# Two matmuls with a gelu between them: the first weight range cast on other engines, one table load, x of three pairs earlier, phase two's reads moved

## The chip, the cores and the metric

One core of a Trainium2 chip. The metric is the device time of one execution in microseconds (us).

## The reference

```python
x: (8, 1024, 1024) float32, w1: (1024, 4096), w2: (4096, 1024)
h = x @ w1
h = 0.5 * h * (1 + np.tanh(np.sqrt(2 / np.pi) * (h + 0.044715 * h ** 3)))
return (h @ w2).astype(np.float32)
```

## The kernel before

**Phase one** makes `gelu(x @ w1)` and writes it in float16 to memory; **phase two** reads it back transposed and multiplies it by w2. All engines run in the order in which the program is written out by hand (a manual schedule): each engine takes its own instructions strictly in that order, and waits where an operand or a buffer isn't ready. Casts to float16 are scaled: a chunk of x by a measure of its rows, a weight range by its largest value.

x is 8192 rows, taken as 64 *chunks* c of 128 rows, two of which make a *pair* k (32 pairs). w1's columns are taken in four *ranges* r; range 0 is loaded as eight *halves* n (`load_w1(0, n)`), of which 0 to 3 belong to one block of columns and 4 to 7 to the other.

A chunk goes through these steps: `load_x`, `look_x` (ScalarE, sums magnitudes, L190), `scale_x` (VectorE, L193 and L197), `cast_x` (L179 on VectorE, L177 on GpSimd), then `turn_x_pe`: eight transposes on TensorE into the PSUM tile `turned` (L216) and a copy from there into `xT[k]` (L221 on ScalarE, L223 on VectorE). A half of w1: `look_w1` (its largest value; VectorE L150, or ScalarE L285), `widest_w1` and `scale_w1` (largest over all halves of a block, through one transpose on TensorE, L162), `cast_w1`. `factors_of_block` makes the few numbers with which products are scaled back.

The first six pairs (FIRST) are multiplied plainly with range 0, the first one also with range 1. This is cut into 28 *quarters* p of 8 matmuls (L401): a half of the pair's rows against one block of columns. Pairs 0 and 1 take quarters 0 to 7, pair 2 takes 8 to 11, pair 3 12 to 15, pair 4 16 to 19, pair 5 20 to 23; 24 to 27 are pair 0 with range 1. After each quarter comes a gelu on ScalarE (L441) and a cast on GpSimd (L177) into a tile `g2`; a store to memory follows on the SP queue when both casts of a tile are made (L450). Steps for later pairs are placed in the quarters by a table, `early(p, step, ...)`: they are emitted after quarter p. The function `between` emits steps in the middle of quarters 0, 1 and 3.

The remaining products of phase one run in *units* (a pair and a range), by a scheme with seven products instead of eight; a unit's methods are m1 to m7 (TensorE) and g21, g11, g22, g12 (gelus). They are spread over three units' time, and each unit has seven slots for background work.

Phase two takes each pair in 26 *products* s, whose left sides are sums (`sum_g`, VectorE, L171) of tiles that DMA transposes bring (`load_g`, L548, on the SP queue), and whose right sides are tiles made from w2 and fetched on the SP queue (L395). `take` reads a product's bank: the first read of an output quarter is ScalarE's (L573), the later ones VectorE's (L569). The last two units of phase one share their time with the first products: `extra()` emits three products, twice in a unit.

Tiles of several kinds (the junk that a look writes, `x16`, `e`, `g2`, the sums `gs`) share one ring of 11 buffers, `k2`, handed out in order of allocation; the casts `g` of the units share 8.

Of the kernel before, what the change touches and what calls it, by code (L numbers as in the profile page):

```python
# [10 lines left out]
ACT = mybir.ActivationFunctionType  # L11
# [68 lines left out]
def kernel(  # L80
# [60 lines left out]
    ratio = small.tile([P, 2], F32, name="ratio")  # L141
# [5 lines left out]
    V, S, G = nc.vector, nc.scalar, nc.gpsimd  # L147

    def absmax(dst, src):
        V.tensor_reduce(  # L150
            out=dst, in_=src, op=ALU.max, axis=AX.X, apply_absolute_value=True
        )
# [20 lines left out]
    def cast(eng, o, i, s):  # L173
        if eng is S:
            S.activation(out=o, in_=i, func=ACT.Copy, scale=s)
        elif eng is G:
            G.tensor_scalar(out=o, in0=i, scalar1=s, scalar2=1.0, op0=ALU.mult, op1=ALU.mult)  # L177
        else:
            V.tensor_scalar(out=o, in0=i, scalar1=s, scalar2=None, op0=ALU.mult)  # L179
# [8 lines left out]
    def look_x(c):  # L188
        junk = k2.tile([P, H], mybir.dt.bfloat16, name="junk", tag="k2")
        S.activation(out=junk, in_=xraw[c], func=ACT.Abs, accum_out=xl[:, c:c + 1])  # L190
# [50 lines left out]
    def times(o, a, s, eng=V):  # L241
        if eng is G:
            G.tensor_scalar(out=o, in0=a, scalar1=s, scalar2=1.0, op0=ALU.mult, op1=ALU.mult)
        else:
            V.tensor_scalar(out=o, in0=a, scalar1=s, scalar2=None, op0=ALU.mult)
# [8 lines left out]
    def factors_of_block(k, block, eng):  # L254

        c, b = slice(2 * k, 2 * k + 2), slice(NR + block, NR + block + 1)
        times(up[:, block, c], xm[:, c], w1m[:, b], eng)
        times(rt[:, c] if block else rs[:, k, :, 0], xi[:, c], w1j[:, b], eng)
# [12 lines left out]
    def load_w1(r, n, pool=wpool, tag="w"):  # L271
        b, half = BLOCKS[n // 2], n % 2
        row = (b in (B21, B22)) * HK * P + half * 2 * P
        col = (b in (B12, B22)) * I // 2 + r * N
        wraw[r, n] = pool.tile([P, 2, N], F32, name="wn", tag=tag)
        (G if r else nc.sync).dma_start(
            out=wraw[r, n],
            in_=w1[row:row + 2 * P, col:col + N].rearrange("(c p) n -> p c n", p=P),
        )

    def look_w1(r, n, eng=V):
        src, dst = wraw[r, n].rearrange("p c n -> p (c n)"), w1c[:, r, n:n + 1]
        if eng is S:
            junk = k2.tile([P, 2 * N], mybir.dt.bfloat16, name="junk", tag="k2")
            S.activation(out=junk, in_=src, func=ACT.Abs, scale=1.0 / SPAN, accum_out=dst)  # L285
        else:
            absmax(dst, src)
# [29 lines left out]
    def cast_w1(r, n, eng):  # L317
        b, half = BLOCKS[n // 2], n % 2
        if (r, b) not in w1set:
            w1set[r, b] = wpool.tile([P, HK, N], F16, name="w", tag="w")  # L320
        c = r or NR + n // 4
        cast(eng, w1set[r, b][:, 2 * half:2 * half + 2], wraw.pop((r, n)), w1i[:, c:c + 1])
# [296 lines left out]
    NQ = len(order)  # L619
    todo = {}  # L620

    def plan(u, slot, f, *args):
        assert 0 <= u, (f, args)
        todo.setdefault((u, slot), []).append((f, args))
# [6 lines left out]
    def early(p, f, *args):  # L631
        plan(p // 4, p % 4, f, *args)

    early(1, turn_x_pe, 3, S)
    for k in range(2, FIRST):
        for h in range(2):
            c = 2 * k + h
            p = (4, 7, 11, 14)[k - 2] + h
            early(p - 1, look_x, c)
            early(p, scale_x, c)  # L640
            early(p, cast_x, c, V)
            if h:
                early(p, factors_of_block, k, 0, V)
                early(p, factors_of_block, k, 1, G)
            if k > 3:
                early((2, 5)[k - 4], load_x, c, wpool, "w")
            early(4 * k - 2 + 2 * h, turn_x_pe, c, V if h else S)
    for k in first:
        for i in range(4):
            if k == 1:  # L650
# [16 lines left out]
    for r in range(2, NR):  # L667
        u = (r - 1) * FIRST - 1
# [24 lines left out]
    for k in list(middle) + list(last):  # L693
        a = at[k] if k in middle else at[last[0]]
        for h in range(2):
            c = 2 * k + h
# [10 lines left out]
    u = at[middle[0]] - 1  # L707
# [22 lines left out]
    for i, node in enumerate(FORMS):  # L730
        r, n = divmod(i, 7)
# [6 lines left out]
    def unit(u, extra):  # L738
        q = now.get(u)
        p1, p2 = now.get(u - 1), now.pop(u - 2, None)  # L740
        if u < NQ:
            q = now[u] = Quad1(*order[u])
            q.m1()
        background(u, 0)
        if p1:
            p1.m7()
        if p2:
            p2.g21()
        if p1:
            p1.g11()  # L750
        let_go(len(held) - 2 if len(held) > 2 else 0)
        if u >= NQ:
            extra()
        background(u, 1)
        if p2:
            p2.m3()
        background(u, 2)
        if u < NQ:
            q.m2()
        background(u, 3)  # L760
        if u < NQ:
            q.m6()
        if p1:
            p1.g22()
        if p2:
            p2.g12()
        let_go(len(held) - 2 if len(held) > 2 else 0)
        background(u, 4)
        if u < NQ:
            q.m5()  # L770
        background(u, 5)
        if p1:
            p1.m4()
        if u >= NQ:
            extra()
        background(u, 6)

    with tc.manual_schedule(
        engines={
            mybir.EngineType.PE, mybir.EngineType.Activation, mybir.EngineType.DVE,  # L780
            mybir.EngineType.Pool, mybir.EngineType.SP,
        }
    ):
        load_x(0, wpool, "w")
        for n in range(4):
            load_w1(0, n)
        make_identity(nc, identity)
        V.tensor_copy(out=identity16, in_=identity)
        for c in range(1, 4):
            load_x(c, wpool, "w")  # L790
        for n in range(4, 8):
            load_w1(0, n)
        for c in range(4, 8):
            load_x(c, wpool, "w")
        look_x(0)
        scale_x(0)
        cast_x(0, S)
        t = x16[0]
        turn_x_pe(0, S)
        warm_up(t, WARM)  # L800
        for n in range(4):
            look_w1(0, n)
        widest_w1(0, 0)
        for c in range(1, 4):
            look_x(c)
        scale_w1(NR)
        warm_up(t, 12)
        cast_w1(0, 0, V)
        cast_w1(0, 1, G)
        scale_x(1)  # L810
        cast_x(1, V)
        cast_w1(0, 3, G)
        cast_w1(0, 2, V)
        factors_of_block(0, 0, G)
        plain = {(k, 0): Plain(k, 0) for k in range(FIRST)}
        plain[0, 1] = Plain(0, 1)
        quarters = [(k, 0, half, s) for s in range(2) for k in range(2) for half in range(2)]
        quarters += [(k, 0, half, s) for k in range(2, FIRST) for half in range(2) for s in range(2)]
        quarters += [(0, 1, half, s) for half in range(2) for s in range(2)]

        def between(p):
            if p == 0:
                turn_x_pe(1, V)
                look_w1(0, 4, S)
                scale_x(2, 2)
                cast_x(2, V)
                cast_x(3, G)
                factors_of_block(1, 0, G)
            elif p == 1:
                turn_x_pe(2, V)  # L830
                look_w1(0, 5, S)
                look_w1(0, 6)
                look_w1(0, 7)
                widest_w1(0, 1)
            elif p == 3:
                scale_w1(NR + 1)
                for n in (4, 5, 6, 7):
                    cast_w1(0, n, G if n % 2 else V)
                for k in range(2):
                    factors_of_block(k, 1, V)  # L840

        for p, (k, r, half, s) in enumerate(quarters):
            plain[k, r].quarter(half, s, ("pa", "pc")[p % 2], lambda: between(p))
            for j in (p % 4,) if p % 4 < 3 else (3, 4, 5, 6):
                background(p // 4, j)
            let_go(len(held) - 1 if len(held) > 1 and p % 2 else 0)
        now = {}
        for u in range(FIRST + 1, NQ):
            unit(u, None)
        V.tensor_scalar(  # L850
            out=vo, in0=xm, scalar1=w2n, scalar2=SPAN, op0=ALU.mult, op1=ALU.mult
        )
        V.tensor_scalar(out=vn, in0=vo, scalar1=-1.0, scalar2=None, op0=ALU.mult)
        for u in range(NQ, NQ + 2):
            unit(u, lambda: second(3))
        let_go()
        for u in range(NQ + 2, NQ + 6):
            for slot in range(7):
                background(u, slot)
        assert not todo, todo.keys()  # L860
        second(NP * len(PRODUCTS) - done[0])
# [28 lines left out]
```

## Time and profile before

| | |
|---|---|
| median of 3 runs | 1542.61 us (1542.05 to 1543.32) |
| profiled execution | 1542.97 us, its span 1541.1 us |
| TensorE busy | 1521.2 us, 99% |
| VectorE, ScalarE, GpSimd busy | 77%, 47%, 32% |
| ScalarE's table loads | 2, of 1.28 us, at 0.74 and 18.29 |
| first product of a quarter | 14.20 us |
| phase two's first product | 806.24 us |

The profile calls TensorE PE (PEld its weight loads), VectorE DVE, ScalarE ACT, GpSimd POOL, SyncE's DMA queue SPq. In a timeline a line has the start, the time from the first start to the last end, the engine, the line of the program, the operation, output <- input with sizes and type, and in brackets how long the engine stood idle before it and what ended that. Ends of matmuls are modelled: starts are exact, so a wait of TensorE is read best from starts.

### The profile page before, as it was taken

The numbers are of one execution on the slowest core, as the hardware profiler recorded it, in microseconds if no ns is written. First come the engines' busy times: TensorE is split into PE (matmuls) and PEld (weight loads), VectorE is DVE, ScalarE is ACT, GpSimd is POOL, SyncE is SP. The second block draws the span as 40 slices with busy tenths as digits, with TensorE's granted clock in tenths as the row PEclk, the third lists the DMA queues.
The fourth block names the chain that finished last, engine by engine and source line by source line (L and its number), as shares of the span: only waits on it lengthen the run. The fifth ranks groups of instructions, "written<-read, shape, count | busy, mean of one in ns | idle before, by whom it ended". The sixth has DMA issues, their size and how long they took to land. (4 is left out here: it accounts for less than half of the span.)

```text
span 1541.1 us, 28626 instructions
## 1 busy us (share of the span) xinstructions
PE 1521.2 (99%) x10408; PEld 1014.7 (66%) x10408; DVE 1181.5 (77%) x2413; ACT 731.6 (47%) x1296; POOL 488.2 (32%) x593
## 2 busy tenths in 40 slices
PE   7999999999999999999999999999999999999999
PEld 4444444444444444444448888888888888888888
DVE  6786787777877777675248888888888888888886
ACT  6778777777777777797662111111111111111111
POOL 5778654566656666554442000000000000000000
PEclk9999999999999999999999999999999999999999
DMA  9654989878788887883699668668767767866872
GB/s 333 225 173 145 267 270 312 248 228 229 233 260 239 244 262 211 251 219 104 216 267 235 136 123 165 129 132 151 142 135 136 151 132 129 165 131 123 157 141 80
DMA packets 459806, 293.93 MB, mean 191 GB/s; under 512 B 333840, under 2 KB 427024, under 8 KB 459664
## 3 DMA queue, kind: packets, MB, share of 16 engines
q1 hardware_dynamic: 456208, 279.52, 71.6%
q0 software_dynamic: 3456, 12.58, 2.6%
q8 instruction: 81, 1.33, 0.4%
q14 instruction: 61, 0.50, 0.1%
HBM read 96.99 MB, written 114.29 MB: 137 GB/s over the span
## 5 line engine op out<-in xcount | busy, mean ns | idle before, releaser
L401 PEld LDWEIGHTS <-gs 128*128 128x128 f16 x4608 | 450.7, 98 | 54.7 <-DVE gs L171 1.4
L177 POOL TENSOR_SCALAR g<-e,rs 128x512 f16<-128x512 f32 x448 | 366.1, 827 | 279.6 <-ACT e L453 240.2
L401 PEld LDWEIGHTS <-xs 128*128 128x128 f16 x1936 | 189.4, 98 | 230.9 <-issue 3.5
L168 DVE TENSOR_TENSOR e<-pc,e 128x512 f32<-128x512 f32 x242 | 161.6, 686 | 204.9 <-ACT e L519 203.5
L401 PEld LDWEIGHTS <-xT 128*128 128x128 f16 x1676 | 163.5, 98 | 201.3 <-issue 4.6
L401 PE MATMUL pa<-w,gs 128*128 128x256 f16 x2304 | 288.3, 273 | 1.2 <-ACT o L573 1.2
L401 PE MATMUL pa<-w,xT 128*128 128x512 f16 x1080 | 256.4, 379 | 5.0 <-ACT xT L221 2.0
L453 ACT ACTIVATE e<-e,us 128x512 f32<-128x512 f32 x363 | 249.2, 719 | 6.8 <-DVE e L168 6.8
L401 PE MATMUL pa<-w,xs 128*128 128x512 f16 x968 | 248.4, 379 | 2.4 <-ACT e L500 2.4
L401 PE MATMUL pc<-w,xs 128*128 128x512 f16 x968 | 248.4, 379 | 0.0
L401 PEld LDWEIGHTS <-gT 128*128 128x128 f16 x2048 | 200.3, 98 | 23.7 <-DMA w<-wd 0.5
L573 ACT ACTIVATE o<-pa,vo 128x256 f32<-128x256 f32 x96 | 45.3, 472 | 332.7 <-PE pa L401 332.7
L401 PE MATMUL pc<-w,gs 128*128 128x256 f16 x1536 | 193.8, 273 | 0.2 <-DMA w<-wd 0.2
L401 PE MATMUL pa<-w,gT 128*128 128x256 f16 x1024 | 132.7, 273 | 0.2 <-DMA w<-wd 0.2
L401 PE MATMUL pb<-w,xT 128*128 128x512 f16 x484 | 124.2, 379 | 0.0
L569 DVE SCALAR_TENSOR_TENSOR o<-pc,vo,o 128x256 f32<-128x256 f32 x160 | 77.0, 482 | 58.5 <-PE pc L401 58.5
L510 ACT COPY e<-pa 128x512 f32<-128x512 f32 x121 | 70.9, 586 | 90.4 <-PE pa L401 85.0
L171 DVE TENSOR_TENSOR gs<-gT,gs 128x1024 f16<-128x1024 f16 x160 | 109.3, 683 | 1.5 <-POOL g L177 0.7
L569 DVE SCALAR_TENSOR_TENSOR o<-pa,vo,o 128x256 f32<-128x256 f32 x192 | 92.0, 480 | 19.6 <-PE pa L401 19.6
L401 PE MATMUL pb<-w,gs 128*128 128x256 f16 x768 | 99.5, 273 | 0.0
L401 PE MATMUL pc<-w,gT 128*128 128x256 f16 x768 | 99.5, 273 | 0.0
L500 ACT COPY e<-pa 128x512 f32<-128x512 f32 x121 | 70.0, 579 | 50.5 <-PE pa L401 50.5
(100 smaller groups left out, 1451.4 us busy)
## 6 DMA issues: line engine op xcount, KB each, us to landing
gd<-g SPq DMA_DIRECT2D x484, 128.0 KB, 3.2
wn<-in_w_dram SPq DMA_DIRECT2D x72, 512.0 KB, 5.5
xn<-in_x_dram SPq DMA_DIRECT2D x64, 512.0 KB, 5.6
out_dram<-o SPq DMA_DIRECT2D x62, 512.0 KB, 3.7
w<-wd SPq DMA_DIRECT2D x25, 512.0 KB, 6.3
wn<-in_w_dram POOLq DMA_DIRECT2D x24, 512.0 KB, 5.7
wd<-wt SPq DMA_DIRECT2D x24, 512.0 KB, 5.1
gd<-g SPq DMA_DIRECT2D x14, 256.0 KB, 5.0
```

The lines of the kernel that those rows point to most:

```text
L168: V.tensor_tensor(out=o, in0=a, in1=b, op=ALU.add)
L171: V.tensor_tensor(out=o, in0=a, in1=b, op=ALU.subtract)
L177: G.tensor_scalar(out=o, in0=i, scalar1=s, scalar2=1.0, op0=ALU.mult, op1=ALU.mult)
L401: nc.tensor.matmul(bank, lhsT=left(i), rhs=right[i], start=start and i == 0, stop=i == n - 1, skip_group_check=True,)
L453: S.activation(out=e, in_=src, func=ACT.Gelu_apprx_tanh, scale=self.u[half][s])
L500: S.copy(self.e11, self.pa)
L510: S.copy(self.e12, self.pa)
L569: V.scalar_tensor_tensor(out=o, in0=ps, scalar=v, in1=o, op0=ALU.mult, op1=ALU.add)
L573: S.activation(out=o, in_=ps, func=ACT.Copy, scale=v)
```

## The change

Five edits. (1) Halves 1 and 3, and later 5 and 7, of w1's range 0 are cast on ScalarE instead of GpSimd; the look at chunk 3 goes behind the first two of these casts, the look at half 4 from ScalarE to VectorE, and the factors of block 1 for pairs 0 and 1 from VectorE to GpSimd. (2) A gelu of two numbers per partition is ScalarE's first instruction. (3) Looks, scales and casts of x are emitted one quarter earlier for pair 3 and two for pairs 4 and 5. (4) The turns of pairs 3 to 5 are emitted one quarter earlier. (5) In the two last units the first group of phase two's products, with its sums, reads, and the DMA transposes that it issues for pair 1, goes ahead of the gelus g21 and g11 and of the stores released with them.

```diff
@@ table of early steps
-            p = (4, 7, 11, 14)[k - 2] + h
+            p = (4, 6, 9, 12)[k - 2] + h
...
-            early(4 * k - 2 + 2 * h, turn_x_pe, c, V if h else S)
+            early(4 * k - 2 + 2 * h - (k > 2), turn_x_pe, c, V if h else S)
@@ def unit
         if p1:
             p1.m7()
+        if u >= NQ:
+            extra()
         if p2:
             p2.g21()
         if p1:
             p1.g11()
         let_go(len(held) - 2 if len(held) > 2 else 0)
-        if u >= NQ:
-            extra()
         background(u, 1)
@@ start
+        V.memset(ratio, 0.0)
+        S.activation(out=ratio, in_=ratio, func=ACT.Gelu_apprx_tanh)
         make_identity(nc, identity)
...
-        for c in range(1, 4):
-            look_x(c)
+        look_x(1)
+        look_x(2)
         scale_w1(NR)
         warm_up(t, 12)
         cast_w1(0, 0, V)
-        cast_w1(0, 1, G)
+        cast_w1(0, 1, S)
         scale_x(1)
         cast_x(1, V)
-        cast_w1(0, 3, G)
+        cast_w1(0, 3, S)
         cast_w1(0, 2, V)
+        look_x(3)
@@ def between
                 turn_x_pe(1, V)
-                look_w1(0, 4, S)
                 scale_x(2, 2)
                 cast_x(2, V)
                 cast_x(3, G)
                 factors_of_block(1, 0, G)
+                look_w1(0, 4)
...
                 for n in (4, 5, 6, 7):
-                    cast_w1(0, n, G if n % 2 else V)
+                    cast_w1(0, n, S if n % 2 else V)
                 for k in range(2):
-                    factors_of_block(k, 1, V)
+                    factors_of_block(k, 1, G)
```

## The prediction

> **What bounds the kernel now.** The page first: part 1 gives TensorE (PE) 99% of the span, part 2 a granted clock of 9 in every slice. So only the time in which PE stands still can be won, and the second view, PE's waits, says where that is (us in total, times, longest):
>
> ```profile
> PE 1521.2 (99%) x10408; PEld 1014.7 (66%) x10408; DVE 1181.5 (77%) x2413; ACT 731.6 (47%) x1296; POOL 488.2 (32%) x593
> ...
> PEclk9999999999999999999999999999999999999999
> ```
>
> ```profile
> PE turned L216 <- ACT x L175: 7.2, 1, 7.2
> PE pa L401 <- ACT e L500: 2.4, 4, 1.0
> PE pa L401 <- ACT xT L221: 2.0, 1, 2.0
> PE pa L401 <- DVE w L179: 1.7, 2, 0.9
> PE pa L401 <- ACT o L573: 1.2, 1, 1.2
> PE pa L401 <- POOL w L177: 1.0, 3, 0.4
> PE pa L401 <- DVE xm L193: 0.3, 1, 0.3
> PE pc L401 <- ACT xT L221: 0.3, 1, 0.3
> PE pc L401 <- DMA w<-wd: 0.2, 1, 0.2
> PE pa L401 <- DMA w<-wd: 0.2, 1, 0.2
> ```
>
> Matmul ends are modelled, so I take the lost time from starts. In the timeline four 512-wide matmuls without a wait take 0.863 us from start to start, eight 1.727, eight transposes 0.437. By these, PE loses 4.2 us in quarters 0 to 4 (14.20 to 28.47), 2.16 ahead of quarter 16, 3.0 at four places in the units (76.55, 93.80, 107.07, 131.88, all on L500's copies), and in phase two 1.36 at 814.57 and 0.39 + 0.40 at 831.54 and 832.81. The first product, at 14.20, is not moved by the change: its cast waits for the same chain of maxima.
>
> The timeline around the largest of these:
>
> ```profile
> 47.56 0.69 ACT L441 ACTIVATE e<-pc,up 128x512 f32<-128x512 f32 x1 [1.71 <-DMA gd<-g]
> 50.79 1.00 ACT L221 COPY xT<-turned 128x1024 f16<-128x1024 f16 x1
> 51.85 1.90 PE L401 MATMUL pa<-w,xT 128*128 128x512 f16 x8 [2.00 <-ACT xT L221]
> ```
>
> ScalarE (ACT) stood 1.71 us for a buffer that a store held, then had a look, a look of w1 and two gelus ahead of the copy that quarter 16 needs.
>
> **First range, quarters 0 to 3.** Before: halves 1 and 3 are cast on GpSimd (POOL) in 1.59 us each, and beside it VectorE's casts take 1.16 and 1.60 instead of the 0.75 of rows without it. After: ScalarE is free at 14.11 (its second look), casts half 1 in 1.15 (L175's rows: 1.15, 1.16) to 15.27, half 3 starts 1.05 later and ends at 16.32; VectorE ends half 2 at 15.85. Quarter 0 ends at 17.08 instead of 18.04: 0.96 ahead. Little of that stays. The look at chunk 3 now stands behind both casts (16.22, before 14.24), VectorE's scale of chunks 2 and 3 waits for it (17.39, before 17.64), and then the look at half 4 (1.21) that ScalarE gave up stands on VectorE ahead of the copy of turned chunk 2: 19.58 to 20.27. Quarter 2 starts at 20.33 instead of 20.66.
>
> The table load (1.28 at 18.29) leaves ScalarE; the built program of the change has one load, at its head, where ScalarE idles until x lands at 4.42 anyway, and that also hides the memset and the 128x2 gelu. Gelu of quarter 0 goes at 17.38, chunk 3's copy ends at 21.69, ahead of the end of quarter 2: quarter 3 starts at 22.06 instead of 22.84. Its first half ends at 22.92, the transpose of the maxima follows at 23.28 (spread is ready at 23.10, as before; it then waited for PE until 23.71), and the casts of halves 4 to 7 start at 24.40 instead of 24.81. VectorE at 0.75 and ScalarE at 1.05 apart have them ready at 25.15, 25.55, 25.82 and 26.60; quarter 4's last two matmuls start at 26.70 instead of 28.04. Lead: 1.34. The four small factors on POOL (0.27 each) lie beside this and end near 25.5; quarter 4's gelu does not ask before 28.24.
>
> **Pairs 3 to 5 sooner.** ScalarE from 26.50: gelu 0.59, look 1.15, in turn: gelu 3, look 4, gelu 4, look 5, gelu 5, look 6 (new here), gelu 6 at 31.72, copy of chunk 4 32.31 to 33.31. Quarter 8 starts at 33.35, before 34.09: the lead shrinks to 0.74, since the look of chunk 6 was put ahead of that copy. Then PE has eight quarters and now five turns, 13.8 + 2.2: quarter 16 could start at 49.36. Is chunk 8 there? Its look comes at 35.9 instead of 41.46, its turn after quarter 13 (45.1). On ScalarE the copy has one wait ahead: the look at w1 (1,3) needs the buffer of pair 2's first half, whose store goes out after quarter 9's cast, at 39.05 (before 40.51). That store took 6.96 before (the gelu at 47.56 above waited for it): 46.0, then look 1.15, gelu 0.59, copy to 48.74. In time by 0.6. Quarter 17 then starts at 51.12, before 54.03: **lead 2.91**. VectorE's copy of chunk 7 is ready at 44.8, wanted at 45.5; that of chunk 9 and ScalarE's of chunk 10 have 2 us to spare. From quarter 17 on each engine has the order of before, and POOL's loads of w1 follow the gelus, so all of it moves with PE; the four waits in the units stay as they are.
>
> **Phase two.** What the timeline shows:
>
> ```profile
> 811.95 0.48 DVE L569 SCALAR_TENSOR_TENSOR o<-pb,vo,o 128x256 f32<-128x256 f32 x1
> 812.46 0.47 ACT L573 ACTIVATE o<-pb,vn 128x256 f32<-128x256 f32 x1 [1.57 <-DVE o L569]
> 812.84 1.32 ACT L453 ACTIVATE e<-e,us 128x512 f32<-128x512 f32 x2
> 813.57 10.88 SPq L548 DMA_TRANSPOSE gT<-gd  x4
> 814.06 0.46 ACT L573 ACTIVATE o<-pa,vo 128x256 f32<-128x256 f32 x1
> 814.57 1.03 PE L401 MATMUL pa<-w,gs 128*128 128x256 f16 x8 [1.20 <-ACT o L573]
> 824.56 1.56 SPq L395 DMA_DIRECT2D w<-wd  x3
> ```
>
> Product 6 waits for product 3's read of its bank (814.06), which stands behind two gelus, which stand behind product 2's second read, which waits for VectorE. Moved ahead of the gelus, the sums of products 1 and 2 ask for buffers that POOL frees one cast (0.8 to 1.1) earlier, so VectorE's read comes at 811.09 (0.86 earlier) and ScalarE's at 811.60. But two more gelus (units' g21 and g11, which ran in the gap at 808.87 and 809.46) now stand between it and product 3's read: four at 0.61, so 811.60 + 0.38 + 2.44 = 814.42, before 814.06. Product 6: **+0.36**. The reads themselves are not the gain; the SP queue is. The four DMA transposes of pair 1 (2.72 each on the queue) now go ahead of two stores, at 810.2, and end at 821.1; stores and the three fetches of w2 follow at 822.3, over 2 us ahead of 824.56. The two waits for `w<-wd` at 831 go: **-0.79**. The two stores held 11 us longer cost nothing: the six casts left write to buffers whose stores stand ahead of the transposes. Net -0.43.
>
> **Sum.** -2.91 - 0.43 = -3.3. The profiled execution took 1542.97, 1.87 over its span of 1541.1: span 1537.8, execution 1539.6; it stood 0.36 above the median, so 1539.3 against 1542.61.
>
> **A rule against it.** Rows: a cast costs ScalarE 1.15 and VectorE 0.75. The Trainium skill (ScalarE: Activation LUTs, Rules for kernel authors) would have multiplies by a constant on VectorE, not ScalarE, which it has up to three times slower. By that rule all four halves go to VectorE: with chunk 1 between them the last ends near 17.2 and quarter 0 near 17.7, 0.6 later than above, so the rows bear the change out here; what is left of the rule is the first rival, a ScalarE too full.
>
> **Rivals.**
> - *ScalarE stays late at pair 4.* It has hardly a gap from 24.4 to 51.8 with four casts (4.4 us) more. If the store of pair 2 lands at 47.47 as before (the loads of w1 ahead of it take the DMA then, share 0.89 in 40 to 50), look, gelu and copy end at 50.2 and quarter 16 waits 0.9: lead 2.0, time 1540.2. For it: that landing was 6.3 to 7.0 us in this stretch. Against: it is issued 1.5 earlier, and loads with it.
> - *Slower: the ring of 11 buffers.* The same wait, but with earlier stores late as well: gelus 10 and 11 and the look of w1 now each wait for a store, in one queue. Every us past 46.6 that pair 2's store lands is a us. At 49.5 (10.4 after issue) the lead is gone and only the 0.4 of phase two is left; at 51 the time is 1543.7, and at 53.1 1545.8, slower by over 0.2%. Against: no store of this stretch took over 7.0.
> - *More.* The units' four waits (3.0 us) shrink by half because ScalarE arrives there with less to do: 1537.8. Against: its order from quarter 17 on is unchanged.
>
> That the change does not do as said is out for the table: the built program shows the one load.
>
> **How the numbers follow.** Forecast 0.55 (its own range 1538.8 to 1539.8), late ScalarE 0.27, more 0.10, slower 0.08 (most of it over 0.2%). 0.2% is 3.1 us, about what a measurement of this kernel tells from no change: the line is at 1539.5, through the forecast's upper part. Faster: four fifths of 0.55, 0.44, and 0.10, less a little for waits I have not seen: 0.52. Slower 0.07, same the rest. Range: from the better case to a late ScalarE that loses 1 us more, 1538.0 to 1541.3.
>
> **What would show it.** Right: one table load; quarter 4's last pair near 26.7, quarter 8 near 33.4 with a wait of 0.5 on L221, no wait ahead of quarter 16, quarter 17 near 51.1; the wait on L573 grown to 1.7, no wait on `w<-wd`. Wrong: L221 still among PE's waits with 1 us or more at pair 4, a lead at quarter 17 under 2, or longer waits on L500.

## The result, and the profile after

The changed kernel took 1540.01 us, the median of 11 runs (1538.6 to 1541.99), beside 1543.16 for 11 runs of the kernel before (1542.05 to 1544.84): a ratio of 0.9979, with an interval of 0.9970 to 0.9989. The same kernel was timed once more with the last experiments: 1541.5 beside 1543.74, ratio 0.9985 (0.9976 to 0.9994). Faster, then, by 2.2 to 3.2 us in the medians. Both intervals lie below 1 and both hold 0.998, so a gain is shown, and a gain of over 0.2% is neither shown nor excluded. Forecast were 1539.3 us, a range of 1538.0 to 1541.3 and a saving of 3.3. The first measurement lies in the range with a saving of 3.15; the second lies 0.2 above it with a saving of 2.24.

The profiled execution took 1539.32 us, 1.82 over its span of 1537.5. PE's busy time is unchanged, and the granted clock shows 9 in every slice, as before:

```profile
PE 1521.2 (99%) x10408; PEld 1015.3 (66%) x10408; DVE 1181.4 (77%) x2411; ACT 732.9 (48%) x1298; POOL 480.6 (31%) x593
```

So it is waits again that have gone. PE's waits after (total, times, longest), complete but for three of 0.2 or 0.3:

```profile
PE turned L216 <- ACT x L175: 7.1, 1, 7.1
PE pa L401 <- ACT e L500: 2.4, 4, 1.1
PE pa L401 <- ACT o L573: 1.2, 1, 1.2
PE pa L401 <- DVE w L179: 0.8, 1, 0.8
PE pa L401 <- ACT e L453: 0.6, 1, 0.6
...
```

The 2.0 us on L221 ahead of quarter 16 and the waits on GpSimd's casts (`POOL w`) and on `w<-wd` are not there; the four on L500 are what they were. New is 0.6 on L453. In the timeline, quarters 8, 16 and 17, and between them ScalarE's look of w1 (1,3) and the copy that quarter 16 needs:

```profile
32.39 1.90 PE L401 MATMUL pa<-w,xT 128*128 128x512 f16 x8
...
44.65 1.06 ACT L285 ACTIVATE junk<-wn 128x1024 bf16<-128x1024 f32 x1
...
46.27 1.00 ACT L221 COPY xT<-turned 128x1024 f16<-128x1024 f16 x1
...
48.77 1.89 PE L401 MATMUL pa<-w,xT 128*128 128x512 f16 x8
50.50 1.89 PE L401 MATMUL pc<-w,xT 128*128 128x512 f16 x8
```

ScalarE's copy of chunk 8 ends at 47.27, 1.5 us ahead of its quarter. In the kernel before, quarter 17 and phase two's first product started at

```profile
54.03 1.89 PE L401 MATMUL pc<-w,xT 128*128 128x512 f16 x8
...
806.24 1.04 PE L401 MATMUL pa<-w,gs 128*128 128x256 f16 x8
```

Quarter 17 leads by 54.03 - 50.50 = 3.53. (A lead is how much sooner a matmul starts than the same one in the kernel before.) Phase two after the change:

```profile
802.75 1.04 PE L401 MATMUL pa<-w,gs 128*128 128x256 f16 x8
...
806.37 12.78 SPq L548 DMA_TRANSPOSE gT<-gd  x4
...
809.63 1.03 PE L401 MATMUL pa<-w,gs 128*128 128x256 f16 x8 [0.62 <-ACT e L453]
...
811.82 1.03 PE L401 MATMUL pa<-w,gs 128*128 128x256 f16 x8 [1.16 <-ACT o L573]
...
819.25 1.00 SPq L458 DMA_DIRECT2D gd<-g  x2
820.35 1.36 SPq L395 DMA_DIRECT2D w<-wd  x3
```

The lead of the first product is 806.24 - 802.75 = 3.49. Products are counted from 0, as `s` is in the program, and a wait "by starts" is the time from one start to the next less the time that this takes without a wait. Product 5 (809.63) now waits, 0.79 by starts, and product 6 (811.82) waits still, so the lead is 2.75 at product 6 (814.57 - 811.82). The fetches of w2 go out at 820.35 instead of 824.56, both waits for `w<-wd` are gone, and the lead is 3.54 again at the product of 829.27, which stood at 832.81.

### The profile page after: what moved, and what is told of

It is laid out like the page before. It is cut to its first block, busy times and chain, and to the rows that moved or that the text cites. A ratio compares the mean times of both kernels' runs of the same rounds, so it can differ in the third digit from the quotient of the medians.

```text
span 1537.5 us, 28627 instructions
## 1 busy us (share of the span) xinstructions
PE 1521.2 (99%) x10408; PEld 1015.3 (66%) x10408; DVE 1181.4 (77%) x2411; ACT 732.9 (48%) x1298; POOL 480.6 (31%) x593
## 3 DMA queue, kind: packets, MB, share of 16 engines
q8 instruction: 81, 1.33, 0.4%
## 4 chain that ended last, share of the span: by engine, by line
PE 95%; ACT 2%; DMA 1%; DVE 1%; issue 1%; SPq 0%; POOL 0%; ACTq 0%; POOLq 0%; DVEq 0%
PE pa L401 50%; PE pc L401 30%; PE pb L401 14%; DMA gd<-g 1%; DMA xn<-in_x_dram 1%; ACT w L175 1%; ACT e L453 0%; DVE w L171 0%; PE turned L216 0%; DVE e L168 0%; POOL g L177 0%; ACT junk L190 0%; ACT e L441 0%; ACT e L500 0%; SPq L276 0%
## 5 line engine op out<-in xcount | busy, mean ns | idle before, releaser
L453 ACT ACTIVATE e<-e,us 128x512 f32<-128x512 f32 x363 | 249.1, 719 | 6.1 <-DVE e L168 6.1
L573 ACT ACTIVATE o<-pa,vo 128x256 f32<-128x256 f32 x96 | 45.3, 472 | 332.7 <-PE pa L401 332.7
L500 ACT COPY e<-pa 128x512 f32<-128x512 f32 x121 | 69.9, 578 | 50.9 <-PE pa L401 50.1
```

The lines of the kernel that those rows point to most:

```text
L453: S.activation(out=e, in_=src, func=ACT.Gelu_apprx_tanh, scale=self.u[half][s])
L500: S.copy(self.e11, self.pa)
L573: S.activation(out=o, in_=ps, func=ACT.Copy, scale=v)
```

## The experiments

The first product starts anywhere from 13.70 to 15.19 in these profiles, since the loads ahead of it land at different times; so leads are counted from it. (Before: quarter 17 starts 39.83 us behind the first product, phase two 792.04.)

| kernel | lead at quarter 17 | lead at phase two | median, us | ratio to before (interval) |
|---|---|---|---|---|
| changed | 3.58 | 3.54 | 1540.01 | 0.9979 (0.9970 to 0.9989) |
| changed, again | 3.09 | 2.71 | 1541.50 | 0.9985 (0.9976 to 0.9994) |
| e1: edits 1 to 4 | 3.19 | 3.17 | 1540.24 | 0.9980 (0.9971 to 0.9989) |
| e2: edit 5 alone | -1.85 | -1.89 | 1544.24 | 0.9999 (0.9990 to 1.0008) |
| e3: edits 3, 4 | 2.06 | 2.01 | 1542.29 | 0.9988 (0.9979 to 0.9997) |
| e4: edits 1, 2 | 2.45 | 2.40 | 1541.93 | 0.9989 (0.9980 to 0.9997) |
| e5: without edit 2 | 2.41 | 2.36 | 1541.40 | 0.9985 (0.9976 to 0.9994) |
| e6: transposes alone of edit 5 | 3.38 | 3.34 | 1540.78 | 0.9982 (0.9973 to 0.9990) |
| e8: edits 1, 2, 4 | 4.45 | 2.47 | 1541.66 | 0.9984 (0.9975 to 0.9994) |
| e9: edits 1, 2, 3 | 3.03 | 2.14 | 1542.43 | 0.9989 (0.9980 to 0.9999) |
| e10: pair 3's looks at old place | 3.63 | 3.53 | 1541.28 | 0.9982 (0.9973 to 0.9991) |
| e11: and a look of w1 later | 3.82 | 2.70 | 1540.79 | 0.9974 (0.9965 to 0.9984) |
| e13: and without edit 5 | 3.19 | 3.12 | 1540.83 | 0.9976 (0.9966 to 0.9986) |

A lead is one execution, a median nine to eleven. The profiled executions of e9 (1547.2), e10 (1544.33) and e5 (1544.23) lie 3 to 5 us above the medians of their kernels. The count from the first product is itself good to some 0.6 us only: in the kernels with edits 1 and 2 quarter 5 follows it after 11.98 to 12.64 us, sooner where the first product came late.

**Taking the change apart.** e1 has edits 1 to 4:

```diff
-        if u >= NQ:
-            extra()
         if p2:
             p2.g21()
...
+        if u >= NQ:
+            extra()
         background(u, 1)
```

> The change without its last edit (phase two's first products go behind the gelus again, as before). Theory: the whole gain is the first range, and phase two's move gives back what it wins. Then quarter 17 starts near 50.5 as with the full change, product 6 waits 1.4 us instead of 0.8 (product 5) and 1.3 (product 6), the two waits of 0.4 for w<-wd come back near 828, and the time is that of the full change, 3.0 to 3.6 us under before. Rival (the prediction's own sum): phase two's move is worth 0.4 us, so this one is 0.4 us slower than the full change.

e2 is the kernel before with edit 5 alone:

```diff
+        if u >= NQ:
+            extra()
         if p2:
             p2.g21()
...
-        if u >= NQ:
-            extra()
         background(u, 1)
```

> The kernel before with the last edit alone. Theory: within 0.15 us of before: the waits for w<-wd (0.8) go, products 5 and 6 wait 0.75 us more. Rival: 0.4 us faster, as the prediction summed it. All of phase one stays as before, quarter 17 at 54.0.

e1 saves 0.20%, e2 nothing. As far as medians with intervals of 1.4 us to either side can tell, the whole change is worth no more than its first range; the 0.4 us between theory and rival is too little for them. In e2's profile the waits for `w<-wd` are all but gone (0.1 by starts) and product 5 waits 0.39, but quarter 17 came at 56.31, not at 54.0: the granted clock fell behind quarter 16 (last section).

e3 is the kernel before with the table of x alone:

```diff
-            p = (4, 7, 11, 14)[k - 2] + h
+            p = (4, 6, 9, 12)[k - 2] + h
...
-            early(4 * k - 2 + 2 * h, turn_x_pe, c, V if h else S)
+            early(4 * k - 2 + 2 * h - (k > 2), turn_x_pe, c, V if h else S)
```

> The kernel before with the looks, casts and turns of pairs 3 to 5 sooner, and nothing else. Theory: the wait ahead of quarter 16 goes (it was ScalarE's order, not its load), quarters 0 to 4 stay as before: quarter 8 near 34.1, quarter 16 near 50.1, quarter 17 near 51.8 instead of 54.0; 2.2 us faster. Rival (ScalarE too full, or the store too late): the wait on L221 moves to quarter 8 or stays at 1 us or more at quarter 16, under 1.2 us faster.

e4 is the kernel before with the casts on ScalarE and the early table load:

```diff
+        V.memset(ratio, 0.0)
+        S.activation(out=ratio, in_=ratio, func=ACT.Gelu_apprx_tanh)
...
-        cast_w1(0, 1, G)
+        cast_w1(0, 1, S)
...
-        cast_w1(0, 3, G)
+        cast_w1(0, 3, S)
         cast_w1(0, 2, V)
+        look_x(3)
...
-                    cast_w1(0, n, G if n % 2 else V)
+                    cast_w1(0, n, S if n % 2 else V)
```

> The kernel before with the first range's casts on VectorE and ScalarE and gelu's table at the start, and nothing else. Theory: quarters 0 to 4 win about 1.5 us (quarter 4's end near 26.9 instead of 28.47), quarter 8 starts about 1.3 us sooner, and the wait ahead of quarter 16 stays and takes part of it, since the look at chunk 8 and the copy keep their places: 0.7 to 1.5 us faster. Rival (the parts don't add, one of them hides the other): this alone wins 2.5 us or more, or nothing.

e4's waits show what the two do to each other:

```profile
PE pa L401 <- ACT xT L221: 1.8, 1, 1.8
```

The wait ahead of quarter 16 hardly shrinks, and yet a lead of 2.28 at quarter 8 arrives at quarter 17 as 2.45. What the copy waits for (gelus, and a store that follows them) is early too, so the lead passes through. e3 takes the same wait away and wins 2.06. Alone the two win 2.06 + 2.45 = 4.5, together 3.1 to 3.6: the look of chunk 6 ahead of the copy of chunk 4 costs quarter 8 0.27 us (it starts 5.62 behind quarter 5 in e4, 5.89 in the changed kernel), and quarter 10 waits 0.33. The other 0.26 between e4 and the changed kernel at quarter 8 (17.61 and 18.14 behind the first product) is there at quarter 5 already.

**Looks or turns.** e8 is e1 with the old places of looks, scales and casts:

```diff
-            p = (4, 6, 9, 12)[k - 2] + h
+            p = (4, 7, 11, 14)[k - 2] + h
```

> Edits (1), (2) and (4), without (3) and (5): the turns of pairs 3 to 5 are sooner, the looks, scales and casts of x stay at their old quarters. Theory (the look decides at quarter 16): quarter 8 has no look of chunk 6 ahead of the copy of chunk 4, so its lead is 0.5 above that of the casts alone or the same (2.3 us, counted from the first product), but the look of chunk 8 still comes late on ScalarE and its copy too: the wait on L221 ahead of quarter 16 stays, 1 to 2 us, and quarter 17 leads by 2.2 to 2.8 us. Rival (the turn decides): the copy of chunk 8 comes one quarter sooner, no wait on L221 is left at quarter 16, and quarter 17 leads by 3.5 or more.

e9 is e1 with the old turns:

```diff
-            early(4 * k - 2 + 2 * h - (k > 2), turn_x_pe, c, V if h else S)
+            early(4 * k - 2 + 2 * h, turn_x_pe, c, V if h else S)
```

> Edits (1), (2) and (3), without (4) and (5): looks, scales and casts of x sooner, the turns at their old quarters. Theory (the look decides at quarter 16): with the look of chunk 8 sooner the copy follows its turn at once; the turn of chunk 8 comes only one quarter ahead of quarter 16, which 1.7 us of quarter covers against 0.6 + 1.0 for turn and copy, so the wait on L221 ahead of quarter 16 is under 0.6, and quarter 17 leads by 3.0 to 3.6 us, counted from the first product, as in the changed kernel. Rival (the turn decides): the wait on L221 stays at 1.5 or more and the lead is 2.5 or less.

In e8 the rival held: quarter 16 has no wait, and the lead of 4.45 is the largest of all. In e9 the theory held (0.2 on L221, 3.03). Either edit alone is enough for the wait in these profiles, one of each; the sooner looks are the dearer way. But e8's larger lead does not last. The timeline further on:

```profile
77.67 1.22 DVE L150 TENSOR_REDUCE w1c<-wn 128x1 f32<-128x1024 f32 x1 [1.16 <-DMA wn<-in_w_dram]
...
81.94 0.33 PE L162 MATMUL rows<-identity,spread 128*128 128x128 f32 x1 [1.55 <-DVE spread L155]
```

At 81.94 PE has waited for the maxima of range 2, after VectorE had to wait for halves of that range to land; with 0.25 at the same step of range 1 (54.68), some 2 us of the lead are gone by phase two. e9 waits 0.90 at this place, too. In the changed kernel this transpose starts at 80.08 without a wait.

**The table load.** e5 is the changed kernel without the memset and the gelu at the start:

```diff
-        V.memset(ratio, 0.0)
-        S.activation(out=ratio, in_=ratio, func=ACT.Gelu_apprx_tanh)
```

> The changed kernel without edit (2): the memset and the first gelu are left out, so that the one table load (1.28 us) falls ahead of the gelu of quarter 0, as before the change. Theory (covered): in the changed kernel ScalarE stood idle 0.22 us ahead of that gelu (17.10), 0.89 ahead of the next (19.71) and 0.61 ahead of the third (21.90). Of the 1.28 a half us reaches the copy of turned chunk 3 (20.29 to 21.30, wanted at 21.62), so quarter 3 starts about 0.2 later, and the wait of 0.76 ahead of quarter 4, which hangs on the maxima of halves 4 to 7, takes that up or not: quarter 17 within 0.4 of the changed kernel's, counted from the first product, and the median within 0.4 us of it. Rival (it was the table): the load moves every later copy by its 1.28, quarter 5 and quarter 17 come 1.0 to 1.3 us later, and a third of the change's gain is edit (2)'s.

The load fell at 17.00 and the first gelu at 18.30 instead of 17.10; quarter 4 starts 10.48 us behind the first product, as against 10.45, and all quarters up to 15 as in the changed kernel. So far the load is covered, as the theory has it. Quarter 17 was not within 0.4 (lead 2.41 against 3.58), and the median, 1541.40, is 1.4 above the changed kernel's first and 0.1 below its second. What cost this execution its lead was something else, further down the timeline:

```profile
47.19 1.06 ACT L285 ACTIVATE junk<-wn 128x1024 bf16<-128x1024 f32 x1 [2.54 <-DMA gd<-g]
...
49.87 1.90 PE L401 MATMUL pa<-w,xT 128*128 128x512 f16 x8 [0.96 <-ACT xT L221]
...
831.81 1.05 PE L401 MATMUL pa<-w,gT 128*128 128x256 f16 x8 [0.70 <-DMA w<-wd]
834.17 1.05 PE L401 MATMUL pc<-w,gs 128*128 128x256 f16 x8 [1.31 <-DMA w<-wd]
```

The look of w1 (1,3) waited for pair 2's store, which was issued at 38.46 and took 8.6 us to land. And the waits for `w<-wd` were there, longer than before the change, with the transposes ahead of the stores all the same: they took 14.23 on the queue.

**Phase two's order.** e6 is e1 with pair 1's transposes alone moved ahead:

```diff
-            if s == 0 and k + 1 < NP:
+            if s == 0 and 0 < k and k + 1 < NP:
...
+        if u == NQ:
+            load_g(1)
         if p2:
             p2.g21()
```

> Edits (1) to (4), and of edit (5) only the DMA transposes of pair 1: they are issued on the SP queue ahead of the gelus g21 and g11 and of the stores, while the first three products with their sums and reads stay behind, as before the change. Theory (two effects that cancel): the transposes ahead end the waits for w<-wd at the products 25 us later, and the reads ahead of the gelus cost 0.74 us at product 5, which waited for the bank of gelu g21. So here no wait for w<-wd, and no wait for ACT e L453 in phase two's first products; from phase two's first product to the thirteenth after it 25.8 to 26.3 us instead of 26.52 in the changed kernel, and 0.3 to 0.7 us less in all, which is too little for the medians. Rival (the products' order does not matter): the same 26.5, with the wait at product 6 alone grown.

No wait for `w<-wd` and none on L453, as expected; but 0.83 by starts at product 2 (VectorE's sum, 0.66 in the wait's own line) and 0.44 at product 3, so 27.33 us for the stretch instead of 26.52. (The stretch, here and in the expectation of e13, runs from product 0 to product 25, 802.75 to 829.27 in the changed kernel; "thirteenth" and "fourteenth" are miscounted.) The expected 26.2 was missed, and the median says nothing.

**The changed kernel again**, with nothing edited:

> The changed kernel again, unaltered, for a second profile and for runs beside the two before. Theory (the store's landing varies from execution to execution): median 1539.5 to 1540.6; in its profile ScalarE's look of w1 (1,3) starts somewhere between 44.6 and 47.3, and quarter 16 waits by what this is past 46.1; the waits for w<-wd near 828 are anything from none to 2 us, as in the kernel without the table load at the start, though the transposes stand ahead of the stores. Rival (these depend on the kernel's order alone): 44.65 again, no wait ahead of quarter 16 and none for w<-wd.

Its timeline:

```profile
46.58 1.06 ACT L285 ACTIVATE junk<-wn 128x1024 bf16<-128x1024 f32 x1 [1.99 <-DMA gd<-g]
...
49.26 1.90 PE L401 MATMUL pa<-w,xT 128*128 128x512 f16 x8 [0.41 <-ACT xT L221]
```

The store was issued at 38.41 and took 8.1 us. With e1 (38.70, 7.5 us) and e6 (38.58, 7.6 us), whose instructions are the same up to phase two, and e5, this makes five executions of one stretch of program: 6.1, 7.5, 7.6, 8.1, 8.6. Quarter 16 starts 2.68 behind that look in both profiles where it waits clearly (49.26 - 46.58, 49.87 - 47.19), so a look by 46.09 costs nothing (48.77 - 2.68), and each us past that is a us. The first profile had the shortest store. The rival (order alone decides) is out; the median of 1541.5 was above the range expected.

**Trying for more.** e10 is the changed kernel with pair 3's looks, scales and casts put back:

```diff
-            p = (4, 6, 9, 12)[k - 2] + h
+            p = (4, 7, 9, 12)[k - 2] + h
```

> All five edits, but the looks, scales and casts of pair 3's chunks stay at their old quarters (7 and 8); those of pairs 4 and 5 are sooner as in the change. Theory: the look of chunk 6 no longer stands ahead of the copy of chunk 4, so quarter 8 and quarter 10 start without a wait, as in the kernel with edits (1), (2) and (4): 0.6 and 0.3 us less. The copy of chunk 8 is then wanted at 47.9 instead of 48.77, and it hangs on a store: three kernels with the same instructions in this stretch had ScalarE's look of w1 start at 44.65, 46.27 and 47.19, because that store took 6.1, 7.6 and 8.6 us. It ends 2.6 after that start, so a start past 45.3 costs. Counted from the first product, the lead at quarter 17 is 4.4 with a quick store and 3.6 or less with a slow one; a further wait at the transpose of range 2's maxima (near 81) cuts it to 3.6 or less, as 1.55 us did in the kernel with edits (1), (2) and (4). The median is within 0.4 of the changed kernel's. Rival: nothing behind takes it back, phase two's first product leads by 4.4 and the median is 0.9 lower.

e11 is e10 with a later look of w1 (1,3):

```diff
-        early((7, 8, 10, 12, 12, 13, 14, 15)[n], look_w1, 1, n, S if n in (3, 5, 7) else V)
+        early((7, 8, 10, 14, 12, 13, 14, 15)[n], look_w1, 1, n, S if n in (3, 5, 7) else V)
```

> As the one before, and the look of w1 (1,3) on ScalarE is emitted after quarter 14 instead of 12, so that it no longer stands ahead of the copy of chunk 8. Theory (the store decides, by the tile that it holds): the next tile of the ring is then asked for by the gelu of quarter 13, which waits for the store in its place; the copy ends 1.6 after the landing instead of 2.6, so a landing up to 46.3 costs nothing, and in most executions no wait is left ahead of quarter 16: the lead at quarter 17 is 4.4 and the runs lie closer together; behind it the transfers of range 2 still cut it to 3.6 or less. Median 0.2 to 0.6 under the kernel before this one. Rival: the look itself is then late for the maxima of range 1, PE waits for spread at 52 to 54, and nothing is won.

In e10 the waits at quarters 8 and 10 are gone; ScalarE then stood idle 2.14 us ahead of a look of x, quarter 16 waited 0.8 by starts, and the lead is the changed kernel's. Its median is 0.2 below that of the changed kernel timed beside it (1541.50). In e11 quarter 16 does not wait: it starts 21.67 us behind quarter 5, as in e8, against 22.27 in the changed kernel. Not as I had put it: ScalarE waited 1.67 ahead of the look of x, not at the gelu of quarter 13. In both the look starts as a store lands: issued at 39.14 and landed after 6.7 us, look at 45.93; 38.22, 6.5 and 44.76. And at 80.36 the maxima of range 2 were 1.08 late, as after e8, so that phase two began at 803.04, no earlier than in the changed kernel. The median is 0.5 below e10's, as expected, but inside the intervals of both. Both profiles have something else as well. The windows of e11 (start, end and length; busy us of PE, PEld, DVE, ACT, POOL; granted clock; DMA share and GB/s):

```profile
812.00:814.00 2.00, 1.35 (x7) 0.97 (x7) 1.53 (x3) 0.97 (x3) 2.00 (x2) 0.54 1.09 190
814.00:816.00 2.00, 2.00 (x13) 1.47 (x12) 1.08 (x2) 0.00 (x0) 0.75 (x2) 0.61 1.08 185
```

Behind its two waits at products 5 and 6 (1.33 and 1.32 by starts) the granted clock was down to 0.54; three products took 4.03 us (812.65 to 816.68) instead of 2.62. This suggested the last run, e11 without edit 5:

```diff
-        if u >= NQ:
-            extra()
         if p2:
             p2.g21()
...
+        if u >= NQ:
+            extra()
         background(u, 1)
```

> The kernel with pair 3's looks at their old quarters and the look of w1 (1,3) after quarter 14, without edit (5): phase two's first products, sums, reads and transposes stand behind the gelus again. Theory (edit (5) loses more often than it wins): with it six profiles took 26.2 to 30.3 us from phase two's first product to the fourteenth product after it (two of them with the granted clock down to 0.5 for some 4 us behind the two waits of 1.2 to 1.4 at products 5 and 6), without it five of six took 26.2 to 27.7 us. Here no wait for ACT e L453, one wait of 1.2 at product 6, no drop of the granted clock at 812 to 820, 26.2 to 27.7 us for the stretch, and a median 0.3 to 1.0 us under that of the same kernel with edit (5) (1540.79), so 1539.8 to 1540.5. Rival (the order of the first products does not matter): the same 1540.8 within 0.3, and the drop of the clock is there too.

No wait on L453, 1.37 at product 6, and the clock stayed at 1.00. But product 2 waited 1.74 for VectorE's sum, product 3 0.31, and the `w<-wd` waits came back with 0.40 and 0.39, so the stretch took 28.63 us and not the 26.2 to 27.7 expected. The median equals e11's, as the rival has it; the drop of the clock, which the rival expected as well, is not there. And quarter 16 waited again, 0.77 by starts:

```profile
46.15 1.06 ACT L190 ACTIVATE junk<-xn 128x1024 bf16<-128x1024 f32 x1 [2.61 <-issue]
```

The store issued at 38.36 took 7.7 us here, so it landed at 46.06. The later look of w1 does not take the store out of quarter 16's way; in e11's profile the store was quick.

## Why the prediction was right, and where not

**The sum was right, its two terms were not.** Forecast 2.91 for the first range and 0.43 for phase two. The first profile has 3.53 and 0.01 (2.75 + 0.79 against 3.53). That the time came out so near is luck in part: 0.62 too little and 0.42 too much largely cancel, and the first profile had the shortest store. The change's gain is the first range's: e1 has it whole, e2 has none that can be told. The prediction's chance of 0.52 for a gain over 0.2% is not settled by the two measurements.

**First range, to quarter 5.** The casts went as told: ScalarE's two in 2.17 from 13.66, VectorE's in 0.75 with no cast on POOL beside them. But from ScalarE's second look on everything ran half a us sooner than forecast. That look began at 12.61, in the kernel before at 12.96 (its x landed sooner, which is nothing of the change), and the cast followed it in 1.05 where 1.15 was taken. VectorE scaled chunks 2 and 3 at 16.91 (forecast 17.39). The term that failed behind this is "spread is ready at 23.10, as before": it was ready at 22.63, since VectorE's looks ahead of it had moved too. So the casts of halves 4 to 7 began at 23.83 (24.40), and quarter 5 at 26.50, not at 27.13, which is 0.43 behind the forecast of 26.70 for quarter 4's last pair: a lead of 1.96, forecast 1.34. The table load, which the working let bring quarter 3 forward, was worth nothing in the changed kernel (e5: quarter 3 starts 7.41 behind the first product, with edit 2 7.37).

**Quarter 8.** Forecast: lead 0.74, so a wait of 0.60 on L221 (1.34 less 0.74). Measured 1.70 and 0.26. The mis-sized term is ScalarE's turn of look and gelu, taken as 1.15 + 0.59; in the trace they follow one another in 1.04 + 0.57 (26.49, 27.53, 28.10). Over three looks and four gelus that is 0.4 less (25.92 to 31.32, forecast 26.50 to 32.31), and with the 0.6 from quarter 5 on it makes the difference. That the look of chunk 6 would cost there was right, and e8 and e10 show it. A wait of 0.3 at quarter 10, on VectorE's copy, was not seen.

**Quarter 16 and the store.** "No store of this stretch took over 7.0" was the step that failed, unnoticed in the first profile, where it took 6.1. In four other profiles of the same instructions it took 7.5 to 8.6, and with 8.1 and 8.6 quarter 16 waited 0.6 and 1.1. So the rival of a late ScalarE, with 0.27 and a landing at 47.47, names what happens in some executions, and a chance was the wrong form for it: it is a spread within one kernel. The landing past which it costs, 46.6 in the rival of the ring, was some 46.0, since quarter 16 could start at 48.77 and not at 49.36.

**Units.** The four waits on L500 stayed at 2.4 us, as forecast. What the first range wins does not always reach phase two, though: at the maxima of range 2 e8, e11 and e9 lost 1.55, 1.08 and 0.90 us, from leads of 4.45, 3.82 and 3.03, and the changed kernel's first profile nothing, from 3.58.

**Phase two.** The forecast had the four gelus ahead of product 3's read, and +0.36 at product 6. It was +0.74: product 5 waits first, for the bank of the gelu g21 that the edit put behind it, a reader that the working did not follow; product 6's own wait on L573 stayed at 1.2 and did not grow to 1.7. The -0.79 for `w<-wd` was there in the first profile, though the transposes took 12.78 and not 10.88, so that w2's fetches went out 0.7 us sooner behind product 0 and not 2. But it was a size taken from one execution: without edit 5 these waits came, by starts, to 0.8, 0.5, 0.6, 0, 0, 2.6 and 0.8 (the kernel before, e1, e3, e4, e8, e9, e13), with it to 0, 0, 2.3, 0, 0 and 0.1 (both profiles of the changed kernel, e5, e10, e11, e2). Mostly smaller, and paid for at product 5: 0.8, 0.2, 0.9, 1.5, 1.3 and 0.4, against none.

Product 2 waits for VectorE's sum in eight of the fourteen profiles, with and without the edit (0.2 to 1.8 us). Behind this, too, stands a store. In the second profile of the changed kernel:

```profile
804.73 1.36 POOL L177 TENSOR_SCALAR g<-e,rs 128x512 f16<-128x512 f32 x2 [3.64 <-DMA gd<-g]
805.46 1.17 DVE L171 TENSOR_TENSOR gs<-gs,gT 128x1024 f16<-128x1024 f16 x1 [1.89 <-POOL g L177]
806.68 1.05 PE L401 MATMUL pb<-w,gs 128*128 128x256 f16 x8 [1.19 <-DVE gs L171]
```

The sum follows a cast on GpSimd, and that cast waited for a store to land. In the eight profiles the cast starts 0.0 to 2.0 us behind product 0, in the six others 0.2 to 0.8 ahead of it. The working had the cast, which frees the buffers that the sums ask for, but not the store that holds the cast up.

**The rule against it.** The Trainium skill (ScalarE: Activation LUTs, Rules for kernel authors) would have the multiplies on VectorE. Four casts there were not tried. What the trace shows speaks for the change: VectorE had no gap from 13.45 to 16.65, while ScalarE, with only the look at chunk 3 put off, cast a half every 1.05 from 13.66.

## What to carry to other kernels

Take the price of a wait that a transfer ends from several profiles: one store of 256 KB, issued at the same place, landed after 6.1 to 8.6 us, and this alone moved the kernel by a us. Where two edits each remove the same wait (here sooner looks and sooner turns), keep the cheaper one. What is won ahead of a step that waits for transfers can be lost there again, here 0.9 to 1.6 us in three of fourteen profiles. Where reads are moved ahead of other work, follow who waits for the bank of what is now behind.

## What the runs showed of the hardware

**Short waits can halve the granted clock.** In e2 PE waited 2.33 us by starts ahead of quarter 16 (2.16 in the wait's own line); the windows behind it:

```profile
52.00:54.00 2.00, 1.55 (x5) 0.61 (x6) 0.63 (x4) 2.00 (x5) 0.27 (x1) 0.68 0.00 0
54.00:56.00 2.00, 2.00 (x9) 0.90 (x8) 1.40 (x3) 1.20 (x4) 1.59 (x3) 0.50 0.00 0
```

Quarter 17 came 3.86 us behind quarter 16 instead of 2.18: 1.7 us on top of the wait. In the kernel before, a wait of 2.16 by starts (2.00 in its line) at the same place left the clock at 1.00. In e10 and e11 two waits with one product of 0.87 us between them did it (1.52 and 1.33, 1.33 and 1.32; 1.66 and 1.41 us lost), in e5 two of 0.92 and 1.32 did not. In windows of 2 us, up to 1536, the granted clock is below 0.97 in these three stretches of the fourteen profiles and nowhere else. The Trainium skill (TensorE: Matmul & The Clock Gate, "Why this matters for your kernels") asks for no gap over about 3 us between bursts of matmuls. By these traces that is too wide: a gap of 2.3, or 2.6 in two pieces, may cost the clock. The same page of the Trainium skill has the gate look at free-running windows of some 3.4 us ("What's actually happening"), which would fit that equal waits do and do not trip it; no run here shows the windows.

**The same transposes took longer when issued ahead of the stores.** Pair 1's four DMA transposes held the SP queue for 10.88 to 11.65 us in the seven profiles that issue them behind the last stores, and for 12.72 to 14.23 in the seven that issue them ahead (both profiles of the changed kernel, e2, e5, e6, e10, e11). Some 2 us of an earlier issue go into this, on a queue where all that follows waits. That the stores are the cause is not shown: pair 2's four transposes, which stand at the same place in every one of the programs, took 11.48 to 13.09 us in the fourteen profiles.
